# Seven products per feed-forward block: two of the weight sums made by accumulating transfers, and the products reordered

## The chip, the cores and the metric

The kernel runs on one core of a Trainium2 chip. The metric is the device time of one execution in microseconds (us), the median of three runs. Smaller is better.

## The reference

Two decoder layers (a gated linear attention and a block-sparse softmax attention) act on one sequence of 256 tokens and 1024 features in float32. Each ends in a SwiGLU feed-forward part, and that part alone is touched by the change:

```python
D_MODEL, SEQ, DEPTH = 1024, 256, 2
FFN_HIDDEN = 2816
def swiglu_ffn(x, w_gu, w_down):
    gate, up = jnp.split(x @ w_gu, 2, axis=-1)
    return (jax.nn.silu(gate) * up) @ w_down
...
x = layer_norm(DEEPNORM_ALPHA * x + swiglu_ffn(x, ffn_w_gu[i], ffn_w_down[i]), ln_g[i, 1], ln_b[i, 1])
```

## The kernel before, in words

**Products in three parts.** Every float32 operand is split into a rounded high half and the rest. ScalarE (ACT) makes the high half with a cast, VectorE (DVE) subtracts it from the raw tile to make the low half, and TensorE (PE) adds three products (high by high, low by high, high by low) into one PSUM bank. So each weight tile of 512 KB (128 partitions by 1024 numbers) costs one transfer, one cast on ACT and one subtraction on DVE before PE may use it. `split_unit` (lines 507 to 511) does this for the blocks of this case.

**Blocks of the feed-forward part.** `ffn` walks the 2816 hidden columns in blocks of the kinds "PSSSSH" (line 654): one plain block of 512 columns, four blocks of 512 columns by `seven` (lines 538 to 618), and one of 256. The four are called blocks 1 to 4 here, by the number b in the code. In each, the two halves of the tokens, the two halves of the 1024 features and the pair gate and up form a product of 2x2 matrices of blocks, and seven products take the place of eight. Each product needs one weight operand of two tiles, q = 0 and 1: the letters A to G in tile names. A is W(0,0) as loaded (the first number is the half of the features, the second 0 for gate and 1 for up), C is W(1,0) and E is W(1,1); the other four are sums. B = A + W(0,1), D = B + W(1,1) and G = D + W(1,0) are made in place in the two tiles named A. F = W(0,1) + W(1,1) is made in the two tiles loaded with W(0,1). Raw tiles other than A are all named X. The left operands are `a00`, `a01` and `a11`, which are pieces of the input, and `s1` to `s4`, which are sums of pieces. The results land in the PSUM banks pa, pc and pb, and move through `keep_` and a few element-wise steps into two tiles e (e1 and e2). PE transposes these (tile tr, lines 607 and 617), and the halves of the transposed tiles (hT) are the left operands of the down-projection (`down_now`, weights d0 to d21, banks fy) of this block, which is issued inside the next block.

**Two ways to add.** `add_to` loads the other operand as raw tiles X and adds with DVE (line 571). `add_dma` (lines 574 to 578) issues a transfer from GpSimd's queue (POOL) that adds what it reads from memory to the tile where it lands (`accum_op`), so that nothing is loaded for that sum alone. Such a transfer must wait until all that read the raw tile before are done.

**What sets the order.** Every step is recorded as an operation with an engine, an estimated duration and the buffers it touches. `Plan.emit` (lines 105 to 188) then walks a model of the five engines: of the operations that are ready it takes the one with the earliest start, then the one recorded earliest, with a small preference for those marked urgent. The result is one fixed order per engine, and each engine works through its own order without overtaking. Big tiles share 41 slots (kind "S"); a load on the SP queue waits until its slot is free. The plan's own estimates set the order alone, never a time on the chip. A load counts 512/330 us of SP's time and lands 2.3 us later (line 235). An accumulating transfer counts 1.3 us of POOL's time and lands 8.0 us later:

```python
    def dma_add(fn, reads, writes, **kw):
        return pl.op("POOL", 1.3, fn, reads, writes, extra=8.0, **kw)
```

**One block, as recorded (lines 580 to 617).** Product a00 with A; DVE adds W(0,1) into A; product s1 with B; two accumulating transfers add W(1,1) into the X tiles of W(0,1); product a01 with C; DVE adds W(1,1) into A; product s2 with D; two rows of tiles of the down-projection of the block before; product s4 with E; transpose of e1; product s3 with F; the other two rows of tiles of the down-projection; DVE adds W(1,0) into A; product a11 with G; transpose of e2. So a block holds six additions on DVE (three sums of two tiles), two accumulating transfers, eight loads of W and four of d.

Of the kernel before, what the change touches and what calls it, by code (L numbers as in the profile page):

```python
# [11 lines left out]
AF = mybir.ActivationFunctionType  # L12
ALU = mybir.AluOpType
# [178 lines left out]
def kernel(ctx, tc, x, positions, gla_w_in, gla_w_gk, gla_b_gk, gla_norm_g, gla_w_out,  # L192
                      moba_w_in, moba_w_out, ffn_w_gu, ffn_w_down, ln_g, ln_b,
                      c_f32, c_i32, out):
    nc = tc.nc
# [16 lines left out]
    pl = Plan(slots)  # L212
# [24 lines left out]
    def act(n, fn, reads, writes, **kw):  # L237
        return pl.op("ACT", 0.16 + 0.00087 * n, fn, reads, writes, **kw)

    def dve(n, fn, reads, writes, fast=False, **kw):  # L240
        return pl.op("DVE", 0.14 + (0.00052 if fast else 0.00097) * n, fn, reads, writes, **kw)
# [5 lines left out]
        return pl.op("PE", cols / 2250.0 + 0.01, fn, reads, writes, **kw)  # L247

    def dma_add(fn, reads, writes, **kw):
        return pl.op("POOL", 1.3, fn, reads, writes, extra=8.0, **kw)  # L250


# [215 lines left out]
    def ffn(i, xs, T, gb, dstT, last, x32):  # L468
# [38 lines left out]
        def split_unit(name, raw):  # L507
            hi, lo = S_(name + "h", True), S_(name + "l", True)
            act(1024, lambda: nc.scalar.copy(hi.r, raw.f), [raw], [hi])  # L509
            dve(1024, lambda: nc.vector.tensor_tensor(out=lo.r, in0=raw.f, in1=hi.f, op=ALU.subtract), [raw, hi], [lo])  # L510
            return hi, lo
# [26 lines left out]
        def seven(b, c0, pend):  # L538


            pa, pc, pb = pl.buf("ps", "pa"), pl.buf("ps", "pc"), pl.buf("ps", "pb")
            e1, e2 = S_("e1"), S_("e2")

            def product(ps, left, ws, first, last_):
                st, rd = lhs(left)
                for q, (wh, wl) in enumerate(ws):
                    def f(q=q, wh=wh, wl=wl):
                        for j in range(2):
                            sh, sl_ = st(2 * q + j)
                            cs = slice(512 * j, 512 * j + 512)  # L550
                            nc.tensor.matmul(ps.f, sh, wh.r[:, cs], start=first and q == 0 and j == 0, stop=False,  # L551
                                             skip_group_check=True)
                            nc.tensor.matmul(ps.f, sl_, wh.r[:, cs], start=False, stop=False, skip_group_check=True)  # L553
                            nc.tensor.matmul(ps.f, sh, wl.r[:, cs], start=False, stop=last_ and q == 1 and j == 1,  # L554
                                             skip_group_check=True)
                    pe(6 * 512, f, rd + [wh, wl], [ps])
# [5 lines left out]
            have = {}  # L562

            def get(kh, gu):
                if (kh, gu) not in have:
                    have[kh, gu] = [load_unit(f"X{q}", unit(kh, gu, q, c0)) for q in range(2)]
                return have[kh, gu]

            def add_to(raws, kh, gu):
                for q, other in enumerate(get(kh, gu)):  # L570
                    dve(1024, lambda q=q, other=other: nc.vector.tensor_tensor(  # L571
                        out=raws[q].f, in0=raws[q].f, in1=other.f, op=ALU.add), [raws[q], other], [raws[q]])

            def add_dma(raws, kh, gu):
                for q in range(2):
                    def f(q=q):
                        nc.gpsimd.dma_start(uv(raws[q]), unit(kh, gu, q, c0), accum_op=ALU.add)  # L577
                    dma_add(f, [raws[q]], [raws[q]])

            ch = [load_unit(f"A{q}", unit(0, 0, q, c0)) for q in range(2)]  # L580
            product(pa, "a00", [split_unit(f"A{q}", ch[q]) for q in range(2)], True, False)
            keep_(pa, e1, 0)
            add_to(ch, 0, 1)
            product(pc, "s1", [split_unit(f"B{q}", ch[q]) for q in range(2)], True, False)
            keep_(pc, e2, 0)
            add_dma(get(0, 1), 1, 1)
            r3 = get(1, 0)
            product(pb, "a01", [split_unit(f"C{q}", r3[q]) for q in range(2)], True, True)
            dve(512, lambda: nc.vector.tensor_tensor(out=e1.f[:, 0:512], in0=pb.f, in1=e1.f[:, 0:512], op=ALU.add),
                [pb, (e1, 0)], [(e1, 0)], urgent=True)  # L590
            act(512, lambda: nc.scalar.activation(e1.f[:, 0:512], e1.f[:, 0:512], AF.Silu), [(e1, 0)], [(e1, 0)],
                table="silu", urgent=True)
            add_to(ch, 1, 1)
            product(pa, "s2", [split_unit(f"D{q}", ch[q]) for q in range(2)], False, False)
            keep_(pa, e1, 1)
            r4 = get(1, 1)
            down_now(pend[:2])
            product(pc, "s4", [split_unit(f"E{q}", r4[q]) for q in range(2)], False, True)
            h, l = S_(f"hT{b}h", True), S_(f"hT{b}l", True)

            def dst(i, cs):
# [3 lines left out]
            dve(512, lambda: nc.vector.tensor_tensor(out=e1.f[:, 0:512], in0=e1.f[:, 0:512], in1=e1.f[:, 512:1024],  # L605
                                                     op=ALU.mult), [(e1, 0), (e1, 1)], [(e1, 0)], urgent=True)
            transpose_split(e1, (h, l), 0, 0, skey=0, dkey=0, dstf=lambda i: dst(i, slice(0, P)))
            product(pa, "s3", [split_unit(f"F{q}", have[0, 1][q]) for q in range(2)], False, False)
            dve(512, lambda: nc.vector.tensor_tensor(out=e2.f[:, 0:512], in0=e2.f[:, 0:512], in1=pa.f,  # L609
                                                     op=ALU.subtract), [pa, (e2, 0)], [(e2, 0)], urgent=True)  # L610
            down_now(pend[2:])
# [509 lines left out]
```

## Time and profile before

| what | value |
|---|---|
| device time, median of 3 runs | 586.07 us (585.33 to 586.32) |
| the profiled execution's own time | 585.35 us |
| its span | 583.6 us |
| PE busy | 572.5 us, 98% |
| DVE busy | 504.6 us, 86% |
| ACT busy | 345.7 us, 59% |
| POOL busy | 42.7 us, 7% |
| granted TensorE clock | 0.997 of full speed (2.4 GHz) |
| bytes moved | 118.30 MB, 203 GB/s |
| loads of X by SP / by POOL, accumulating | 48 / 16, 512 KB each |

The span is the time from the first to the last instruction of the profiled execution; 1.75 us of the execution's own time lie around it. "Busy" counts the time in which an engine had at least one instruction under way. Matmuls overlap (one of 512 columns is under way for 0.39 us, and the next starts 0.23 us later), so a lost moment on PE shows in the distance between the starts of two matmuls more surely than in the busy share. The four blocks of seven products lie at about 139 to 263 us in the first layer and at about 422 to 547 us in the second.

### The profile page before, as it was taken

Reading aid. Unit: us, or ns where it says so; the run is one execution under the profiler, and the core shown is the slowest. Engines: PE = TensorE matmul, PEld = TensorE weight load, DVE = VectorE, ACT = ScalarE, POOL = GpSimd, SP = SyncE. Lnnn points to the kernel's source line nnn. Section 1 sums busy time; section 2 is a strip of 40 time slices with the busy share of each in tenths; the row PEclk is TensorE's granted clock in tenths of the full one; section 3 lists DMA queues with packets and bytes.
Section 4 is the critical chain, followed back from the end, with each engine's and each line's share of the span. In section 5 each row is a group of like instructions: output and inputs, shape, how many; then the busy total and the mean of one; then the engine's idle time right before and its main releaser. Section 6 shows DMA issues by size and latency. Waiting matters only on the chain.

```text
span 583.6 us, 8048 instructions
## 1 busy us (share of the span) xinstructions
PE 572.5 (98%) x3004; PEld 488.4 (84%) x3004; DVE 504.6 (86%) x626; ACT 345.7 (59%) x457; POOL 42.7 (7%) x39
## 2 busy tenths in 40 slices
PE   9999999999999999999999999999999999999994
PEld 8898888888878888889889999788888788888983
DVE  5899467698999999999894789888989999999926
ACT  5886465345858586876353365634595767586410
POOL 1015000010010101000000000000101000010001
PEclk9999999999999999999999999999999999999998
DMA  9984286348797877887376545626867787978201
GB/s 291 344 301 168 74 263 242 109 126 239 247 222 219 259 240 240 219 301 249 103 245 199 153 149 166 216 73 216 212 202 223 206 285 177 316 177 291 78 0 72
DMA packets 56377, 118.30 MB, mean 203 GB/s; under 512 B 5217, under 2 KB 9729, under 8 KB 56338
## 3 DMA queue, kind: packets, MB, share of 16 engines
q1 hardware_dynamic: 51554, 108.81, 55.9%
q0 software_dynamic: 4352, 8.39, 8.8%
q10 hardware_dynamic: 432, 0.59, 0.3%
q8 instruction: 23, 0.38, 0.3%
q14 instruction: 16, 0.13, 0.1%
HBM read 116.72 MB, written 1.05 MB: 202 GB/s over the span
## 4 chain that ended last, share of the span: by engine, by line
PE 75%; DVE 12%; DMA 6%; issue 3%; ACT 2%; DVEq 0%; SPq 0%; ACTq 0%
PE fy L303 6%; PE fy L301 6%; PE fy L302 6%; PE pa L554 3%; PE pa L553 3%; PE pa L551 3%; DMA d0r<-in_ffn_w_down 2%; PE y L303 2%; PE y L301 2%; PE y L302 2%; PE tr L316 2%; DVE A L571 2%; PE pc L554 2%; PE pc L551 2%; PE pc L553 2%
## 5 line engine op out<-in xcount | busy, mean ns | idle before, releaser
L571 DVE TENSOR_TENSOR A<-A,X 128x1024 f32<-128x1024 f32 x48 | 57.2, 1219 | 0.0
L577 POOL DMA_DIRECT2D X<-in_ffn_w_gu x16 | 19.6, 1263 | 206.4 <-DVE e L609 63.7
L325 ACT CAST xT<-tr 128x512 fp32r<-128x512 f32 x16 | 9.2, 590 | 32.2 <-PE tr L316 32.1
L372 POOL TENSOR_TENSOR st<-st,mhalf 128x1 f32<-128x1 f32 x8 | 7.6, 956 | 260.3 <-DVE st L370 260.3
L509 ACT CAST B0h<-A 128x1024 fp32r<-128x1024 f32 x8 | 8.4, 1053 | 9.3 <-DVE A L571 9.2
L360 DVE SCALAR_TENSOR_TENSOR r<-xn,fy 128x512 f32<-128x512 f32 x8 | 5.5, 686 | 9.7 <-PE fy L303 9.7
L509 ACT CAST C0h<-X 128x1024 fp32r<-128x1024 f32 x8 | 8.4, 1052 | 8.8 <-DMA X<-in_ffn_w_gu 8.8
L329 DVE TENSOR_TENSOR xT<-tr,xT 128x512 fp32r<-128x512 f32 x16 | 10.8, 685 | 1.3 <-ACT xT L325 0.7
L614 ACT ACTIVATE e<-pa 128x512 f32<-128x512 f32 x8 | 4.8, 599 | 11.8 <-PE pa L554 11.7
L509 ACT CAST A0h<-A 128x1024 fp32r<-128x1024 f32 x8 | 8.4, 1051 | 5.5 <-DMA A<-in_ffn_w_gu 5.4
L364 DVE BATCH_NORM_STATS2 st<-r 128x6 f32<-128x512 f32 x16 | 11.1, 693 | 0.5
L316 PEld LDWEIGHTS tr<-ident,e 128*128 128x128 f32 x64 | 7.6, 140 | 4.7 <-DVE e L615 1.9
L316 PE MATMUL tr<-ident,e 128*128 128x128 f32 x64 | 9.8, 275 | 1.7 <-DVE e L615 1.0
L382 DVE SCALAR_TENSOR_TENSOR xn<-r,st,lnb 128x512 f32<-128x512 f32 x16 | 11.3, 746 | 0.0
L509 ACT CAST C1h<-X 128x1024 fp32r<-128x1024 f32 x8 | 8.4, 1051 | 4.8 <-DMA X<-in_ffn_w_gu 4.4
L378 DVE SCALAR_TENSOR_TENSOR r<-r,st,lng 128x512 f32<-128x512 f32 x16 | 11.2, 744 | 0.0
L509 ACT CAST G0h<-A 128x1024 fp32r<-128x1024 f32 x8 | 8.4, 1050 | 4.5 <-DVE A L571 4.5
L934 DVE SCALAR_TENSOR_TENSOR og<-o,ss,sg 128x256 f32<-128x256 f32 x8 | 3.6, 478 | 8.5 <-ACT sg L896 8.5
L509 ACT CAST D0h<-A 128x1024 fp32r<-128x1024 f32 x8 | 8.4, 1053 | 3.1 <-DVE A L571 3.1
L560 ACT COPY e<-pa 128x512 f32<-128x512 f32 x16 | 9.3, 580 | 1.0 <-PE pa L554 0.9
L510 DVE TENSOR_TENSOR G1l<-A,G1h 128x1024 fp32r<-128x1024 f32 x8 | 9.8, 1222 | 0.1
L509 ACT CAST A1h<-A 128x1024 fp32r<-128x1024 f32 x8 | 8.4, 1052 | 2.4 <-DMA A<-in_ffn_w_gu 2.4
(1050 smaller groups left out, 2283.2 us busy)
## 6 DMA issues: line engine op xcount, KB each, us to landing
X<-in_ffn_w_gu SPq DMA_DIRECT2D x48, 512.0 KB, 5.0
A<-in_ffn_w_gu SPq DMA_DIRECT2D x16, 512.0 KB, 4.4
X<-in_ffn_w_gu POOLq DMA_DIRECT2D x16, 512.0 KB, 7.5
lng<-in_ln_g SPq DMA_DIRECT2D x4, 512.0 KB, 3.8
lnb<-in_ln_b SPq DMA_DIRECT2D x4, 512.0 KB, 6.1
x<-in_x SPq DMA_DIRECT2D x4, 256.0 KB, 4.6
fg00r<-in_ffn_w_gu SPq DMA_DIRECT2D x2, 512.0 KB, 7.0
fg01r<-in_ffn_w_gu SPq DMA_DIRECT2D x2, 512.0 KB, 8.3
```

The source lines that it names most:

```text
L301: nc.tensor.matmul(ps, lh, rh, start=start, stop=False)
L302: nc.tensor.matmul(ps, ll, rh, start=False, stop=False)
L303: nc.tensor.matmul(ps, lh, rl, start=False, stop=stop)
L316: nc.tensor.transpose(ps.f[:, j * P:(j + 1) * P], src.f[:, k * P:(k + 1) * P], ident.f)
L378: nc.vector.scalar_tensor_tensor(out=r.f[:, sl], in0=r.f[:, sl], scalar=st.f[:, 12:13], in1=g.f[:, sl], op0=ALU.subtract, op1=ALU.mult)
L382: nc.vector.scalar_tensor_tensor(out=xn.f[:, sl], in0=r.f[:, sl], scalar=st.f[:, 15:16], in1=b.f[:, sl], op0=ALU.mult, op1=ALU.add)
L509: act(1024, lambda: nc.scalar.copy(hi.r, raw.f), [raw], [hi])
L551: nc.tensor.matmul(ps.f, sh, wh.r[:, cs], start=first and q == 0 and j == 0, stop=False, skip_group_check=True)
L553: nc.tensor.matmul(ps.f, sl_, wh.r[:, cs], start=False, stop=False, skip_group_check=True)
L554: nc.tensor.matmul(ps.f, sh, wl.r[:, cs], start=False, stop=last_ and q == 1 and j == 1, skip_group_check=True)
L571: dve(1024, lambda q=q, other=other: nc.vector.tensor_tensor(out=raws[q].f, in0=raws[q].f, in1=other.f, op=ALU.add), [raws[q], other], [ra ...
L577: nc.gpsimd.dma_start(uv(raws[q]), unit(kh, gu, q, c0), accum_op=ALU.add)
```

## The change

In each of the eight blocks:

- W(0,1) is no longer loaded by itself. Once A is split, two accumulating transfers add W(0,1) into the A tiles, which gives B. The two additions on DVE that did this are gone.
- F is made the other way round: W(1,1), loaded once for E and for D, is split for E first, and then two accumulating transfers add W(0,1) to it. The old two, which added W(1,1) to W(0,1), are gone. So a block has four accumulating transfers instead of two, four additions on DVE instead of six, and two loads on SP fewer. W(0,1) is still read from memory, now twice and always by an accumulating transfer; the bytes read stay the same.
- The order of recording changes: product a01 with C stands before product s1 with B, and product s4 with E before the first half of the down-projection. Two element-wise steps on e1 (the addition of pb, and Silu) lose their urgent mark.
- The plan gets, for each accumulating transfer, an operation on SP of 2.4 us that issues nothing, reads nothing and writes nothing. It moves the plan's clock of SP, and so the order; the program holds no instruction for it.

```diff
     def dma_add(fn, reads, writes, **kw):
+        pl.op("SP", 2.4, lambda: None)
         return pl.op("POOL", 1.3, fn, reads, writes, extra=8.0, **kw)
...
             keep_(pa, e1, 0)
-            add_to(ch, 0, 1)
+            add_dma(ch, 0, 1)
+            product(pb, "a01", [split_unit(f"C{q}", raw) for q, raw in enumerate(get(1, 0))], True, True)
+            dve(512, lambda: nc.vector.tensor_tensor(out=e1.f[:, 0:512], in0=pb.f, in1=e1.f[:, 0:512], op=ALU.add),
+                [pb, (e1, 0)], [(e1, 0)])
+            act(512, lambda: nc.scalar.activation(e1.f[:, 0:512], e1.f[:, 0:512], AF.Silu), [(e1, 0)], [(e1, 0)],
+                table="silu")
+            r4 = get(1, 1)
             product(pc, "s1", [split_unit(f"B{q}", ch[q]) for q in range(2)], True, False)
             keep_(pc, e2, 0)
-            add_dma(get(0, 1), 1, 1)
-            r3 = get(1, 0)
-            product(pb, "a01", [split_unit(f"C{q}", r3[q]) for q in range(2)], True, True)
...
             add_to(ch, 1, 1)
+            r4s = [split_unit(f"E{q}", r4[q]) for q in range(2)]
+            add_dma(r4, 0, 1)
             product(pa, "s2", [split_unit(f"D{q}", ch[q]) for q in range(2)], False, False)
             keep_(pa, e1, 1)
-            r4 = get(1, 1)
+            product(pc, "s4", r4s, False, True)
             down_now(pend[:2])
-            product(pc, "s4", [split_unit(f"E{q}", r4[q]) for q in range(2)], False, True)
...
-            product(pa, "s3", [split_unit(f"F{q}", have[0, 1][q]) for q in range(2)], False, False)
+            product(pa, "s3", [split_unit(f"F{q}", r4[q]) for q in range(2)], False, False)
```

Line numbers of the changed kernel are one higher than before from line 250 on, but for the steps that the change moves.

**How the order on PE moves.** PE from the end of block 1's product G to block 2's product D, first layer, before (the first matmul of each group of six; tr takes e2 of block 1):

```order
L551 MATMUL pa_1614<-A0h_1464,xT_0_1086 128x512
...
L551 MATMUL pa_1614<-A1h_1475,xT_0_1086 128x512
...
L316 MATMUL tr_1635<-ident,e_0_1409 128x128 x4
L551 MATMUL pc_1644<-B0h_1548,s1hl_1228 128x512
...
L551 MATMUL pc_1644<-B1h_1572,s1hl_1228 128x512
...
L551 MATMUL pb_1665<-C0h_1528,xT_0_1086 128x512
...
L551 MATMUL pb_1665<-C1h_1538,xT_0_1086 128x512
...
L551 MATMUL pa_1614<-D0h_1622,s2hl_1250 128x512
```

And now:

```order
L552 MATMUL pa_1598<-A0h_1490,xT_0_1089 128x512
...
L552 MATMUL pa_1598<-A1h_1502,xT_0_1089 128x512
...
L552 MATMUL pb_1623<-C0h_1521,xT_0_1089 128x512
...
L317 MATMUL tr_1633<-ident,e_0_1426 128x128 x4
L552 MATMUL pb_1623<-C1h_1536,xT_0_1089 128x512
...
L552 MATMUL pc_1651<-B0h_1596,s1hl_1228 128x512
...
L552 MATMUL pc_1651<-B1h_1610,s1hl_1228 128x512
...
L552 MATMUL pa_1598<-D0h_1647,s2hl_1252 128x512
```

C moved ahead of B, and the transpose six matmuls later, into the middle of C.

**How the order on DVE moves, at the end of block 1.** DVE up to the two steps on e1 that the transpose of e1 needs (lines 603 and 605 before, 604 and 606 now), before:

```order
L266 TENSOR_TENSOR d2l_1449<-d2r_1405,d2h_1433 128x1024
L266 TENSOR_TENSOR d3l_1462<-d3r_1421,d3h_1447 128x1024
L571 TENSOR_TENSOR A_0_1127<-A_0_1127,X_0_1260 128x1024
L571 TENSOR_TENSOR A_0_1132<-A_0_1132,X_0_1263 128x1024
L510 TENSOR_TENSOR A0l_1496<-A_0_1444,A0h_1464 128x1024
L510 TENSOR_TENSOR G0l_1506<-A_0_1127,G0h_1484 128x1024
L510 TENSOR_TENSOR G1l_1508<-A_0_1132,G1h_1498 128x1024
L510 TENSOR_TENSOR A1l_1518<-A_0_1451,A1h_1475 128x1024
L603 TENSOR_TENSOR e_0_1373<-pc_1377,e_0_1373 128x512
L605 TENSOR_TENSOR e_0_1373<-e_0_1373 128x512
```

And now:

```order
L572 TENSOR_TENSOR A_0_1141<-A_0_1141,X_0_1190 128x1024
L511 TENSOR_TENSOR G0l_1447<-A_0_1126,G0h_1430 128x1024
L511 TENSOR_TENSOR F1l_1462<-X_0_1285,F1h_1452 128x1024
L604 TENSOR_TENSOR e_0_1380<-pc_1395,e_0_1380 128x512
L606 TENSOR_TENSOR e_0_1380<-e_0_1380 128x512
L267 TENSOR_TENSOR d2l_1488<-d2r_1405,d2h_1460 128x1024
L267 TENSOR_TENSOR d3l_1498<-d3r_1424,d3h_1472 128x1024
L511 TENSOR_TENSOR G1l_1504<-A_0_1141,G1h_1476 128x1024
L511 TENSOR_TENSOR A0l_1514<-A_0_1438,A0h_1490 128x1024
L511 TENSOR_TENSOR A1l_1531<-A_0_1450,A1h_1502 128x1024
```

The two steps on e1 moved ahead of d2, d3, G1 and the splits of the next block's A.

**How the order on DVE moves, at the start of block 2.** What follows the ten rows above, now (line 616 is the step on e2 that the transpose of e2 needs; before, lines 571 to 615, the additions stood where the waiting for B stands now):

```order
L511 TENSOR_TENSOR C0l_1547<-X_0_1486,C0h_1521 128x1024
L610 TENSOR_TENSOR e_0_1426<-e_0_1426,pa_1344 128x512
L511 TENSOR_TENSOR C1l_1556<-X_0_1500,C1h_1536 128x1024
L511 TENSOR_TENSOR E0l_1566<-X_0_1512,E0h_1564 128x1024
L511 TENSOR_TENSOR E1l_1582<-X_0_1529,E1h_1580 128x1024
L511 TENSOR_TENSOR B0l_1606<-A_0_1438,B0h_1596 128x1024
L616 TENSOR_TENSOR e_0_1426<-e_0_1426 128x512
L511 TENSOR_TENSOR B1l_1621<-A_0_1450,B1h_1610 128x1024
L572 TENSOR_TENSOR A_0_1438<-A_0_1438,X_0_1512 128x1024
L572 TENSOR_TENSOR A_0_1450<-A_0_1450,X_0_1529 128x1024
```

C and E are split ahead of B; line 616 stands behind B0l, which now follows a transfer that adds.

## Rows read from the trace of the kernel before

**Rows 1.** The page, busy time of each engine

```profile
PE 572.5 (98%) x3004; PEld 488.4 (84%) x3004; DVE 504.6 (86%) x626; ACT 345.7 (59%) x457; POOL 42.7 (7%) x39
```

**Rows 2.** Windows, one per block of the first layer; columns named in its first line

```profile
core 0: us, PE busy (x) PEld busy (x) DVE busy (x) ACT busy (x) POOL busy (x), PEclk, DMA share, GB/s
139.00:170.00 31.00, 30.40 (x139) 24.92 (x138) 28.65 (x30) 21.89 (x25) 2.41 (x2) 1.00 0.73 221
...
201.50:232.40 30.90, 30.90 (x142) 25.56 (x141) 30.86 (x32) 21.30 (x25) 2.44 (x2) 1.00 0.80 236
```

**Rows 3.** Waits of PE: engine, line, releaser: total us, times, longest

```profile
PE tr L316 <- DVE e L615: 1.0, 2, 0.6
PE tr L316 <- DVE e L605: 0.6, 1, 0.6
```

**Rows 4.** Timeline of PE: start us, us under way, around the four transposes

```profile
162.27 0.39 PE L303 MATMUL fy<-d2l,hT0h 128*128 128x512 f32 x1
163.25 0.63 PE L316 MATMUL tr<-ident,e 128*128 128x128 f32 x4 [0.60 <-DVE e L605]
...
173.06 0.39 PE L554 MATMUL pa<-A1l,xT 128*128 128x512 f32 x1
174.04 0.33 PE L316 MATMUL tr<-ident,e 128*128 128x128 f32 x1 [0.60 <-DVE e L615]
...
445.77 0.39 PE L303 MATMUL fy<-d2l,hT0h 128*128 128x512 f32 x1
446.23 0.30 PE L316 MATMUL tr<-ident,e 128*128 128x128 f32 x1
...
456.21 0.39 PE L554 MATMUL pa<-A1l,xT 128*128 128x512 f32 x1
457.02 0.33 PE L316 MATMUL tr<-ident,e 128*128 128x128 f32 x1 [0.42 <-DVE e L615]
```

**Rows 5.** Timeline of PE: spacing in the stream, and a transpose that waits for nothing

```profile
150.25 0.39 PE L301 MATMUL fy<-d0h,hT0h 128*128 128x512 f32 x1
...
155.69 0.39 PE L551 MATMUL pc<-E0h,s4hl 128*128 128x512 f32 x1
...
158.41 0.39 PE L551 MATMUL pa<-F0h,s3hl 128*128 128x512 f32 x1
...
235.66 0.39 PE L554 MATMUL pa<-A1l,xT 128*128 128x512 f32 x1
235.89 0.60 PE L316 MATMUL tr<-ident,e 128*128 128x128 f32 x4
236.25 0.48 PE L551 MATMUL pc<-B0h,s1hl 128*128 128x512 f32 x1
```

**Rows 6.** Timeline of DVE ahead of the first late transpose

```profile
152.61 1.22 DVE L266 TENSOR_TENSOR d2l<-d2r,d2h 128x1024 fp32r<-128x1024 f32 x1
153.74 1.22 DVE L266 TENSOR_TENSOR d3l<-d3r,d3h 128x1024 fp32r<-128x1024 f32 x1
...
161.69 0.69 DVE L603 TENSOR_TENSOR e<-pc,e 128x512 f32<-128x512 f32 x1
162.41 0.69 DVE L605 TENSOR_TENSOR e<-e 128x512 f32<-128x512 f32 x1
```

**Rows 7.** The page, group of the additions on DVE and of the accumulating issues

```profile
L571 DVE TENSOR_TENSOR A<-A,X 128x1024 f32<-128x1024 f32 x48 | 57.2, 1219 | 0.0
L577 POOL DMA_DIRECT2D X<-in_ffn_w_gu x16 | 19.6, 1263 | 206.4 <-DVE e L609 63.7
```

**Rows 8.** The page, DMA queues: packets, MB, share of 16 engines

```profile
q1 hardware_dynamic: 51554, 108.81, 55.9%
q0 software_dynamic: 4352, 8.39, 8.8%
```

**Rows 9.** DMA issues by window, us to landing: 131 to 135, 447 to 449, 449 to 452

```profile
X<-in_ffn_w_gu POOLq DMA_DIRECT2D x1, 512.0 KB, 9.6
...
d4r<-in_ffn_w_down SPq DMA_DIRECT2D x1, 512.0 KB, 3.2
X<-in_ffn_w_gu POOLq DMA_DIRECT2D x1, 512.0 KB, 6.8
...
X<-in_ffn_w_gu POOLq DMA_DIRECT2D x2, 512.0 KB, 8.1
d5r<-in_ffn_w_down SPq DMA_DIRECT2D x1, 512.0 KB, 7.3
```

**Rows 10.** Timeline: an accumulating pair on POOL and the DVE pair it followed

```profile
227.37 2.35 DVE L571 TENSOR_TENSOR A<-A,X 128x1024 f32<-128x1024 f32 x2
...
229.23 2.44 POOL L577 DMA_DIRECT2D X<-in_ffn_w_gu  x2 [29.74 <-DVE A L571]
```

**Rows 11.** Tile B0h: the cast, duration ns min/median/max

```profile
L509 ACT CAST B0h<-A x8: 1049/1054/1055, 126.6 to 511.7; 128x1024 fp32r<-128x1024 f32 x8
```

More of the change, by code (lines that the diff above doesn't have):

```diff
@@ L582, in seven @@
             keep_(pa, e1, 0)
-            add_to(ch, 0, 1)
+            add_dma(ch, 0, 1)
[5 more added lines that the diff above has]
+            r4 = get(1, 1)
             product(pc, "s1", [split_unit(f"B{q}", ch[q]) for q in range(2)], True, False)
             keep_(pc, e2, 0)
-            add_dma(get(0, 1), 1, 1)
-            r3 = get(1, 0)
-            product(pb, "a01", [split_unit(f"C{q}", r3[q]) for q in range(2)], True, True)
[L589 to L592, printed above, removed]
             add_to(ch, 1, 1)
+            r4s = [split_unit(f"E{q}", r4[q]) for q in range(2)]
+            add_dma(r4, 0, 1)
             product(pa, "s2", [split_unit(f"D{q}", ch[q]) for q in range(2)], False, False)
             keep_(pa, e1, 1)
-            r4 = get(1, 1)
+            product(pc, "s4", r4s, False, True)
             down_now(pend[:2])
-            product(pc, "s4", [split_unit(f"E{q}", r4[q]) for q in range(2)], False, True)
             h, l = S_(f"hT{b}h", True), S_(f"hT{b}l", True)
```

## Prediction

> **What bounds the kernel now.** I read the busy times first: PE is busy for 572.5 of 583.6 us [rows 1], so the most that any edit beside PE's own work can win is what PE loses. The windows by block show who stands nearest to it: in block 3 PE is busy for all of 30.90 us and DVE for 30.86, while the DMA engines are busy for 0.80 of it, all at full clock [rows 2]. So PE sets the pace, DVE runs at the same pace without a pause, and the transfers have a fifth of their time left. The waits of PE then tell where DVE holds PE up: only at transposes of e, 1.0 and 0.6 us in all [rows 3]. The timeline gives the true size of these losses. In the stream 24 matmuls take 155.69 - 150.25 = 5.44 us, so one takes 0.227 us [rows 5], and a transpose that waits for nothing starts 0.23 us after the matmul ahead of it and lets the next one start 0.36 us later [rows 5]. The four late transposes start 0.98, 0.98, 0.46 and 0.81 us after theirs [rows 4]: 0.75 + 0.75 + 0.23 + 0.58 = 2.3 us lost. All four lie in block 1 of a layer or at its end. For the first of them DVE shows why: its instructions follow each other without a break from d2 at 152.61 to line 605 at 162.41 [rows 6], although product E, which line 603 needs, ended when F began at 158.41 [rows 5], some 3 us before line 603. So at most 2.3 us (0.4%) of this stage can be won by relief of DVE; 0.2% (1.17 us) is about what a measurement of this kernel tells from no change.
>
> **What the change takes away.** Sixteen additions on DVE, two per block. One lasts 1.22 us [rows 7] and the next starts 1.13 us after it (153.74 - 152.61, a subtraction of the same shape [rows 6]), so a block's DVE work falls by 2.3 us, from 30.9 to 28.6. None of it is on PE's path except where the four transposes wait. Sixteen loads on SP go too; SP issues the rest earlier or waits for slots as before, and I price that at nothing, since loads lead their use by several us.
>
> **What it adds: DMA time.** The queue shares price a transfer. Plain: 55.9% of 583.6 us for 108.81 MB [rows 8], which is 3.0 us per MB and 1.57 us for 512 KB. Accumulating: 8.8% for 8.39 MB [rows 8], 6.1 us per MB, 3.21 us for 512 KB. A block held 12 plain and 2 accumulating ones: 18.8 + 6.4 = 25.3 us, 0.82 of 30.9, against 0.80 read [rows 2]. It will hold 10 and 4: 15.7 + 12.8 = 28.5 us, 0.92. That is still under PE's 30.9, so by itself it costs nothing; its cover is the fifth of DMA time that was idle, and most of this cover goes. POOL issues four times 1.26 us [rows 7] in 30.9; nothing else is queued there inside the blocks, and the steps of the layer norm stand before and after them in POOL's order. The casts on ACT and the matmuls stay the same in number.
>
> **What it adds: a wait.** B now needs an accumulating transfer where it needed an addition of 1.22 us. The order says what lies in front and behind; block 2 has the least room. Let PE start its A at time 0. Between the end of block 1's E and time 0 PE has d0 and d1, a transpose, F, d2 and d3, and G: 72 matmuls and 0.36 us, 16.7 us. DVE goes through two steps on e1 (0.7 us each), d2, d3, G1 and A0 (1.13 us each) after E, 5.9 us; with 0.3 us for the hand-over, which is my choice, A0 is split at -10.5. POOL starts 0.64 us after the DVE instruction that frees the tile (229.23 less 227.37 and 1.22 [rows 10]), at -9.9. On the other side, D must be ready when PE has done A, C, a transpose and B: 36 matmuls and 0.36 us, at 8.5. From B0l on, DVE has five instructions of 1.13 us (B0l, B1l, two additions, D0l) and three short ones of 0.7 us: 7.8 us. So B0l must start by 0.7, and with the cast before it (1.05 us [rows 11]) the first transfer must have landed by -0.3: **9.6 us after its issue**. The rows have landings of 6.8 us, 8.1 as the middle of a pair, and 9.6 at the worst [rows 9]. I take 8.1, as the new transfers are pairs too. That leaves 1.5 us, and the wait costs PE nothing. The range is kept from 6.8 (2.8 us left) upward.
>
> The Trainium skill would leave more room: "DMA: Bandwidth & Descriptors", section "Anatomy of one DMA — SWDGE (gpsimd) path", fits 2.0 us plus the bytes at 436 GB/s for a transfer of GpSimd's queue, an estimate of 3.2 us for 512 KB. By that the wait would be over 6 us early and the first rival below would have no chance. The rows [rows 9] are two to three times as long, and I go by them.
>
> **The moved steps.** Between E and the transpose of e1 stood F and half of d2, 18 matmuls, 4.1 us; now it is d0 and d1, 5.4 us, and its two steps stand ahead of d2, d3, G1 and A on DVE. The transpose of e2 had A, 12 matmuls; now it has 18, 4.1 us, but line 616 stands behind B0l. E now follows B with only D between (2.7 us), and adds into the bank from which ACT must first copy B's result; that copy stands behind the cast of d4 on ACT. d4 landed 3.2 us after its issue [rows 9], and I price this at nothing. The empty operation of 2.4 us on SP issues nothing. Since it depends on nothing, the plan can place it wherever SP would wait, at the start of the program too; it may shift transposes outside the blocks. I take 0, with bounds of -0.3 and +0.8 us (the worst single late transpose [rows 4]).
>
> **The sum.** The four late transposes go: -2.3 us; I leave 0.3 of it for hand-overs, so -2.0. The profiled execution took 585.35 us and would take 583.35. The median of the runs shown, 586.07, is 0.72 above that execution, so the forecast is **584.1 us**. PE's stream cannot shrink further, so this case reaches from 583.0 to 584.9.
>
> **Rivals.** *The transfers for B land late (slower).* Place: B0l of blocks 2 and 4 in both layers; it decides from 9.6 us after issue. Block 4 has twelve instructions on DVE between A0l and B0l and is about as tight; block 3 has some 2 us more. Two accumulating transfers beside one plain load need 2 x 3.21 + 1.57 = 8.0 us of the engines, and such a trio landed at 8.1 and 7.3 us [rows 9], so they do share. Beside three plain loads it would be 2 x 3.21 + 3 x 1.57 = 11.1 us, 1.5 us too late, four times: +6.0 - 2.0 = +4.0, 590.1 us. For it: 0.92 of DMA time is close to full, and d5 took 7.3 us beside accumulating transfers where d4 took 3.2 [rows 9]. Against it: two loads per block are gone from just the stretch ahead of B. The Trainium skill speaks for it: "DMA: Bandwidth & Descriptors", section "Issuing engines are not separate DMA queues", says that transfers issued by GpSimd interleave with all others on the same 16 engines. The trace agrees in the trio just named.
>
> *Half the gain (no change).* B0l lands in time for D but holds line 616 back, so the transposes of e2 stay late (0.75 + 0.58) and only those of e1 go: -1.0, 585.1 us. For it: line 616 stands right behind B0l. Against it: it has 18 matmuls of cover where it had 12. To this case belongs that DVE's relief is eaten by idling at B0l.
>
> *The change isn't what it says.* The empty operations change the order far from the blocks. Price 0 to +0.8, inside the cases above.
>
> **How the numbers follow.** The gain of 2.0 gets 0.46, the half gain or none 0.27, the late transfers 0.27; these are also the chances of faster, same and slower by the 0.2% named above. I put the forecast highest because the chain has 1.5 us left by the rows and DVE gains 2.3 us per block, but no higher, because all that can be won is 2.3 us while each microsecond of lateness is paid four times or more. The range goes from 583.0 (all 2.3 us won, and a run 0.7 below the median, as the lowest was) to 590.1 (the late transfers at their price), which leaves out rather less than 2 in 10.
>
> **What would show it.** Right: DVE busy for about 28.6 us of a block with pauses ahead of B0l, additions 32 instead of 48, PE without waits at transposes of e, DMA share near 0.92, accumulating landings of 7 to 9 us. Wrong: PE waiting for D, B or E, or ACT waiting at B0h for a DMA while PE stands; landings of 10 us and more; or blocks of more than 31 us.

## The result, and the profile after

The changed kernel took **589.34 us** (median of eight runs, 586.79 to 592.14); the kernel before, run beside it eight times, took 585.50. The ratio is 1.0072, with a 95% interval of 1.0050 to 1.0093: slower by 3.8 us, where 584.1 was forecast. The profiled execution took 588.89 us, with a span of 587.1, 3.5 us more than before.

Four things came out as forecast: the work of DVE, the price of a transfer, the DMA share and the four transposes. The page of the changed kernel has the engines' busy times, the group of the additions, and the DMA queues (packets, MB, share of 16 engines):

```profile
PE 573.4 (98%) x3004; PEld 488.6 (83%) x3004; DVE 488.3 (83%) x610; ACT 343.1 (58%) x457; POOL 62.0 (11%) x55
...
q1 hardware_dynamic: 47202, 100.42, 50.7%
q0 software_dynamic: 8704, 16.78, 17.3%
...
L572 DVE TENSOR_TENSOR A<-A,X 128x1024 f32<-128x1024 f32 x32 | 38.5, 1220 | 0.1
```

The additions fell from 48 to 32 and DVE's busy time by 16.3 us [rows 1, 7]. An accumulating transfer takes 17.3% of 587.1 us, divided by 32, which is 3.17 us of the 16 engines; 3.21 was forecast [rows 8]. The windows from product A on, one per block of layer 1, answer to [rows 2]: DVE has 28.51 us on average where it had 30.9, the DMA share is 0.84 to 0.97, and PE loses 0.26 us in 123.6:

```profile
core 0: us, PE busy (x) PEld busy (x) DVE busy (x) ACT busy (x) POOL busy (x), PEclk, DMA share, GB/s
139.50:170.40 30.90, 30.90 (x142) 25.58 (x141) 27.77 (x28) 18.93 (x22) 3.64 (x3) 1.00 0.87 236
170.40:201.30 30.90, 30.90 (x142) 25.58 (x141) 29.66 (x29) 21.48 (x25) 4.85 (x4) 1.00 0.84 231
201.30:232.20 30.90, 30.64 (x139) 25.04 (x138) 27.89 (x29) 21.33 (x25) 4.81 (x4) 1.00 0.97 241
232.20:263.10 30.90, 30.90 (x141) 25.46 (x140) 28.71 (x30) 24.64 (x29) 2.41 (x2) 1.00 0.91 276
sum 123.60, PE 123.34 PEld 101.66 DVE 114.03 ACT 86.39 POOL 15.71; mean PE 30.83 PEld 25.41 DVE 28.51 ACT 21.60 POOL 3.93
```

The four late transposes of [rows 4] are on time. So the gain is in this execution: from the start of A in block 1 to its start in block 3, PE takes 61.78 us in layer 1 and 62.54 in layer 2, where the kernel before takes 63.38 and 63.24, which is 2.3 us less. What took it back stands, for the most part, in the first of these rows of PE's waits (engine, line, releaser: total us, times, longest); the second is two other transposes, of e2 of blocks 2 and 4 in layer 1:

```profile
PE pc L552 <- ACT e L561: 2.7, 1, 2.7
...
PE tr L317 <- DVE e L616: 0.8, 2, 0.5
```

The first row is product E of block 3 in layer 2. PE's timeline there (start us, us under way, engine, line, output and inputs; in brackets the idle time and what ended it):

```profile
497.22 0.39 PE L304 MATMUL fy<-d8l,hT2h 128*128 128x512 f32 x1
500.31 0.80 PE L552 MATMUL pc<-E0h,s4hl 128*128 128x512 f32 x1 [2.70 <-ACT e L561]
500.90 0.63 PE L554 MATMUL pc<-E0h,s4hl 128*128 128x512 f32 x1
501.33 0.63 PE L555 MATMUL pc<-E0l,s4hl 128*128 128x512 f32 x1
...
503.03 0.60 PE L552 MATMUL pc<-E1h,s4hl 128*128 128x512 f32 x1
503.46 0.41 PE L554 MATMUL pc<-E1h,s4hl 128*128 128x512 f32 x1
503.71 0.40 PE L555 MATMUL pc<-E1l,s4hl 128*128 128x512 f32 x1
```

The first matmul of E starts 3.09 us after the one ahead of it instead of 0.23. The next seven distances are 0.59 and then 0.43 us, not 0.23: 512 columns in 0.43 us is the lower of the clock's two levels, 1.2 GHz. They take 3.15 us, 1.5 more than at full speed. Then PE runs at 0.23 again. The windows say the same of the clock:

```profile
490.00:500.00 10.00, 7.61 (x34) 5.94 (x32) 8.77 (x9) 6.36 (x9) 1.20 (x1) 1.00 0.92 264
500.00:510.00 10.00, 9.69 (x36) 7.88 (x37) 8.89 (x10) 6.53 (x8) 2.44 (x2) 0.83 0.85 213
```

So one wait costs 2.9 + 1.5 = 4.4 us. The starts of product A in blocks 3 and 4 agree. They are 35.6 us apart now:

```profile
484.59 0.40 PE L552 MATMUL pa<-A0h,xT 128*128 128x512 f32 x1
...
520.19 0.40 PE L552 MATMUL pa<-A0h,xT 128*128 128x512 f32 x1
```

They were 31.15 us apart before:

```profile
485.45 0.40 PE L551 MATMUL pa<-A0h,xT 128*128 128x512 f32 x1
...
516.60 0.40 PE L551 MATMUL pa<-A0h,xT 128*128 128x512 f32 x1
```

The span is 3.5 us longer: 4.4 us here, less the 2.3 won, and 1.4 us outside the blocks named so far, 0.6 of it ahead of block 1 of layer 1 and 0.8 from block 3 of layer 1 to block 1 of layer 2.

ACT's timeline in block 3 of layer 2 shows why the copy of B's result (line 561) came so late:

```profile
493.04 0.63 ACT L588 ACTIVATE e<-e 128x512 f32<-128x512 f32 x1 [0.86 <-DVE e L586]
495.88 1.05 ACT L266 CAST d11h<-d11r 128x1024 fp32r<-128x1024 f32 x1 [2.21 <-DMA d11r<-in_ffn_w_down]
496.84 1.04 ACT L510 CAST G0h<-A 128x1024 fp32r<-128x1024 f32 x1
497.79 1.04 ACT L510 CAST F0h<-X 128x1024 fp32r<-128x1024 f32 x1
498.73 1.04 ACT L510 CAST D1h<-A 128x1024 fp32r<-128x1024 f32 x1
499.68 0.58 ACT L561 COPY e<-pc 128x512 f32<-128x512 f32 x1
```

ACT stood 2.2 us for d11, and its order has three more casts ahead of the copy. B had ended with the matmul of 495.86. The load of d11 went out at 487.82, 1.7 us behind the first accumulating transfer for F (486.15), and landed 8.0 us later; before, d11 took 3.3. In block 3 of layer 1 of the changed kernel d11 landed after 3.2 us, ACT had one cast and not three between d11's and the copy, and E, six matmuls behind B there too, did not wait. The page's list of DMA issues (KB each, median us to landing) shows the same of the weights:

```profile
X<-in_ffn_w_gu SPq DMA_DIRECT2D x32, 512.0 KB, 5.8
A<-in_ffn_w_gu SPq DMA_DIRECT2D x16, 512.0 KB, 6.4
A<-in_ffn_w_gu POOLq DMA_DIRECT2D x16, 512.0 KB, 7.3
X<-in_ffn_w_gu POOLq DMA_DIRECT2D x16, 512.0 KB, 7.8
```

Before, the two kinds of SP's loads had 5.0 and 4.4.

This is one execution. In the eight runs time and mean granted clock go together: 586.79 us at 0.996, 592.14 us at 0.988. A difference of 0.008 over 588 us is 4.7 us of work at full speed, most of the 5.35 between these two, which suggests that how often the clock falls differs from run to run. The three executions at 0.995 or more took 586.8 to 588.0, so 1.3 to 2.5 us of the loss are there without these falls.

### The profile page after: what moved, and what is told of

Read it like the earlier page. It is cut to its first block, busy times and chain, and to the rows that moved or that the text cites. A ratio compares the mean times of both kernels' runs of the same rounds, so it can differ in the third digit from the quotient of the medians.

```text
span 587.1 us, 8042 instructions
## 1 busy us (share of the span) xinstructions
PE 573.4 (98%) x3004; PEld 488.6 (83%) x3004; DVE 488.3 (83%) x610; ACT 343.1 (58%) x457; POOL 62.0 (11%) x55
## 3 DMA queue, kind: packets, MB, share of 16 engines
q0 software_dynamic: 8704, 16.78, 17.3%
## 4 chain that ended last, share of the span: by engine, by line
PE 45%; DVE 4%; DMA 3%; ACT 2%; issue 1%; DVEq 0%; ACTq 0%
PE fy L304 4%; PE fy L302 4%; PE fy L303 4%; PE pa L555 2%; PE pa L554 2%; PE pa L552 2%; DMA d11r<-in_ffn_w_down 1%; DMA A<-in_ffn_w_gu 1%; PE tr L317 1%; PE mq L302 1%; PE mk L302 1%; PE mk L303 1%; PE mq L304 1%; PE mk L304 1%; PE mq L303 1%; PE v L302 1%
## 5 line engine op out<-in xcount | busy, mean ns | idle before, releaser
L572 DVE TENSOR_TENSOR A<-A,X 128x1024 f32<-128x1024 f32 x32 | 38.5, 1220 | 0.1
L578 POOL DMA_DIRECT2D A<-in_ffn_w_gu x16 | 19.5, 1264 | 100.2 <-DVE A0l L511 67.4
L510 ACT CAST B0h<-A 128x1024 fp32r<-128x1024 f32 x8 | 8.4, 1050 | 12.8 <-DMA A<-in_ffn_w_gu 12.2
L511 DVE TENSOR_TENSOR F1l<-X,F1h 128x1024 fp32r<-128x1024 f32 x8 | 9.8, 1221 | 3.1 <-ACT F1h L510 3.1
L511 DVE TENSOR_TENSOR B0l<-A,B0h 128x1024 fp32r<-128x1024 f32 x8 | 9.8, 1223 | 1.9 <-ACT B0h L510 1.9
L510 ACT CAST D1h<-A 128x1024 fp32r<-128x1024 f32 x8 | 8.4, 1050 | 4.9 <-DVE A L572 4.7
L511 DVE TENSOR_TENSOR A0l<-A,A0h 128x1024 fp32r<-128x1024 f32 x8 | 9.8, 1221 | 1.3 <-ACT A0h L510 1.3
L511 DVE TENSOR_TENSOR F0l<-X,F0h 128x1024 fp32r<-128x1024 f32 x8 | 9.8, 1220 | 0.7 <-ACT F0h L510 0.7
```

The costliest lines, as they stand in the source:

```text
L572: dve(1024, lambda q=q, other=other: nc.vector.tensor_tensor(out=raws[q].f, in0=raws[q].f, in1=other.f, op=ALU.add), [raws[q], other], [ra ...
```

## The experiments

**The theories.** One: the time is lost where PE's E waits behind a copy on ACT, and in the clock after it. Two: the accumulating transfers take the DMA engines' time from the loads, wherever the lateness then comes out. Three: the empty operations on SP spoil the order. Each result is set against the runs of the kernel before that were made beside it (585.1 to 585.6 us).

### Moving the copy, halving the transfers, leaving out the empty operations, E late

*e1: one instruction of ACT moved; all else keeps its order.* Of the finished order, the copy of block 3 in layer 2 is taken ahead of four casts:

```diff
-        for o in order:
+        for o in hoist(self, order, (6,), 4):
             for b in o.made:
...
```

> The changed kernel with one instruction moved on one engine: in block 3 of layer 2 ACT copies B's result (line 561) ahead of the casts of d11, G0, F0 and D1 instead of behind them; every other engine keeps its order. Theory one (the time went at this place: E waits for a copy that stands behind a late load on ACT, and the clock falls after the pause): the row of PE's product E waiting for ACT line 561, 2.7 us, goes; D1 may wait in its place, at most about 1.5 us, since its cast now follows the copy; with a clock that stays full the time is 585 to 587, against 589.3 of the changed kernel. Theory two (the transfers as such cost the time, everywhere): no change, 588.5 to 590. Theory three (the empty operations and the plan's order): no change either.

Measured: 588.92 us (+3.6). The row of E is gone, and others have come (waits of PE):

```profile
PE tr L317 <- DVE e L616: 1.7, 3, 0.9
...
PE pa L555 <- DVE D1l L511: 0.7, 1, 0.7
PE tr L317 <- DVE e L606: 0.7, 1, 0.7
...
PE pa L552 <- ACT D1h L510: 0.4, 1, 0.4
```

The last three lie within 11 us of E's start: D1's cast now comes behind the copy and d11's, and the transpose of e1 is late in turn. From A to A this block still takes 34.05 us. The first row lies, but for 0.16 us, in other blocks. So the copy alone is not the cause: ACT is late as a whole, and PE waits at whichever instruction it needs next. Theory one falls in its narrow form.

*e2: each accumulating transfer moves half of its rows, in the same order.*

```diff
-                        nc.gpsimd.dma_start(uv(raws[q]), unit(kh, gu, q, c0), accum_op=ALU.add)
+                        nc.gpsimd.dma_start(uv(raws[q])[:, 0:1], unit(kh, gu, q, c0)[:, 0:1], accum_op=ALU.add)
```

> The changed kernel with the same order of instructions, but each accumulating transfer of lines 582 and 596 moves half of its rows, 256 KB instead of 512; so A and F hold only half of their second weights, and everything behind them is computed from that. Theory one (d11 lands late because it shares the DMA engines with the accumulating pair): d11 lands after 3 to 5 us instead of 8.0, ACT's wait of 2.2 us for it goes, E's wait falls from 2.7 us to 0.7 at most, and the time is 583.5 to 585. Rival (the order alone is too tight, wherever d11 lands): E still waits 2 us or more and the time stays above 588.

Measured: 583.68 us (ratio 0.9968 to 1.0003). With not one instruction moved, the changed kernel's surplus of 3.8 us is gone, and 1.6 us more. ACT's timeline at the same place:

```profile
492.17 1.03 ACT L266 CAST d11h<-d11r 128x1024 fp32r<-128x1024 f32 x1
...
495.96 0.57 ACT L561 COPY e<-pc 128x512 f32<-128x512 f32 x1
```

The same casts run without a pause, the copy is in time, and PE has no wait for E. Seen from the start of A, d11's cast is 3.0 us earlier: the load landed after 5.9 us, not 8.0 (3 to 5 were expected), and it went out 1.1 us earlier. So in this order the bytes of the transfers decide, as theory two says.

*e3: no empty operations.*

```diff
     def dma_add(fn, reads, writes, **kw):
-        pl.op("SP", 2.4, lambda: None)
```

> The changed kernel without the empty operation on SP. In its order block 3 of layer 1 gets what block 3 of layer 2 has: the casts of d11, G0, F0 and D1 ahead of the copy of B's result. Theory one: the wait and the fall of the clock, 4.4 us together in the changed kernel, come twice, or at least in both layers in part: 590 to 594. Rival (the empty operations cost time through the order they give): faster than the changed kernel, 587 or less.

Measured: 589.59 us (+4.3), near the changed kernel and just under the range of theory one. E waits in four blocks, two of each layer, without a fall of the clock (0.997 in this execution):

```profile
PE pc L551 <- ACT e L560: 3.4, 4, 1.1
```

*e4: E behind the first half of the down-projection, as before.*

```diff
-            product(pc, "s4", r4s, False, True)
             down_now(pend[:2])
+            product(pc, "s4", r4s, False, True)
```

> The changed kernel with product E recorded behind the first half of the down-projection again, as it was before; both accumulating transfers and the order C, B stay. Theory one (E too close behind B): at least 18 matmuls, 4 us, stand between B and E, no wait of E for line 561, no fall of the clock in the blocks, 583.5 to 585. Theory two (the accumulating transfers): 587 or more, with PE waiting for B, D or F behind a transfer.

Measured: 585.08 us, ratio 1.0001 (0.9983 to 1.0019): no wait for E, and the loss is gone with full transfers too. By the medians, so is the gain. The profiled execution (584.22 us, 0.9 below the median) shows the gain: from A of block 1 to A of block 4 the two layers together take 2.6 us less than before. About 1.3 us come back outside, 1.2 of them as a wait of PE for a transpose (line 616) behind block 4 of layer 1. *e8* is the same without the empty operations:

> Product E recorded late and no empty operations on SP: the order of the blocks is nearly the same in both layers. If the empty operations are worth nothing: 585.1, as with them, within 0.7. If they cost something through the order far from the blocks: 584.2 or less, which would be faster than before.

Measured: 585.10 us (0.9970 to 1.0016). The empty operations are worth nothing that can be told; theory three falls.

### E's place and the transfers, apart

*e5: the new order alone, the sums as before.*

```diff
-            add_dma(ch, 0, 1)
+            add_to(ch, 0, 1)
...
-            add_dma(r4, 0, 1)
+            add_dma(get(0, 1), 1, 1)
...
```

> Only the new order of the products: C before B, E straight behind D; the sums are made as before (W(0,1) loaded, two additions on DVE for B, one accumulating pair for F), so a block holds 12 plain and 2 accumulating transfers, 25.3 us, and 48 additions again. Theory one (E early costs only where transfers land late and hold ACT up): E waits for line 561 0.5 us in all at most, DVE is full again and some transposes of e are late, and the time is that of before within 1 us, 584.5 to 586.5. Rival (E early costs by itself): E waits for line 561 in several blocks, 2 us and more in all, and the time is 588 or more.

Measured: 588.61 us (+3.3, 1.0033 to 1.0066). The rival won: E early can cost with a DMA share of 0.79 and 0.75 (blocks of layers 1 and 2) too. But this is not the changed kernel's order: the plan put E0 straight behind B1 in four of the eight blocks, where the changed kernel has 6 to 18 matmuls between them. These are the four where PE waits, 3.1 us in all:

```profile
PE pc L552 <- ACT e L561: 3.1, 4, 1.0
```

PE's timeline at the first of them, then ACT's:

```profile
179.18 0.39 PE L555 MATMUL pc<-B1l,s1hl 128*128 128x512 f32 x1
180.33 0.50 PE L552 MATMUL pc<-E0h,s4hl 128*128 128x512 f32 x1 [0.77 <-ACT e L561]
```

```profile
179.17 0.63 ACT L588 ACTIVATE e<-e 128x512 f32<-128x512 f32 x1 [0.52 <-DVE e L586]
179.71 0.57 ACT L561 COPY e<-pc 128x512 f32<-128x512 f32 x1
```

Here the copy stands behind an activation that waits for DVE, which is full again. *e11* has the edits of e4 and e5, so E is recorded late:

> Of the whole change only C before B, with two additions on DVE and loads as before, and E recorded late: 25.3 us of transfers and 30.9 us of DVE per block. If the exchange of C and B costs and gains nothing by itself: 585.3 as before, within 0.7. If C before B is what makes DVE or ACT late: 587 or more.

Measured: 591.44 us (+5.9). Neither reading fits: the plan still put E0 straight behind B1 in the same four blocks, and E waits there for 4.9 us in all. So this pair does not say what C before B costs alone, nor what E's place costs in the changed kernel's own order. It does say that recording a step late doesn't place it late.

*e7: E late, transfers halved (the edits of e2 and e4).*

> Product E recorded late, as in the run before, and each accumulating transfer of lines 582 and 596 with half of its rows (A and F hold half of their second weights). With E late the changed kernel took 585.1, with half transfers and E early 583.7. If the full transfers still cost something with E late: 583 to 584.3, faster than before. If E's place was all: 585.1 as with full transfers, within 0.5.

Measured: 583.26 us, ratio 0.9967 (0.9945 to 0.9990), 2.0 us faster than before: the first reading, that the full transfers still cost something with E late, 1.8 us against e4. The profiled executions of e4 and e7 have spans of 582.4 and 582.3 us, so no trace shows where these 1.8 lie. That stays open.

*e6: the new pair into A alone; F as before.*

```diff
-            add_dma(r4, 0, 1)
+            add_dma(get(0, 1), 1, 1)
...
```

> The changed order with the new accumulating pair into A alone; F is made as before from a load of W(0,1) and an accumulating W(1,1). A block then holds 12 plain and 4 accumulating transfers, 12 x 1.57 + 4 x 3.21 = 31.7 us of the DMA engines beside 30.9 us of PE, and 32 additions. Theory one (the engines' time decides): the DMA share of the blocks reaches 0.97 or more, loads land late everywhere, PE waits behind casts in most blocks, and the time is 590 to 600. Rival (E's place decides and the transfers don't): as the changed kernel, 587 to 590, or less.

Measured: 595.24 us (+10.0), inside the first range. The DMA share of layer 1's blocks is 0.87 to 0.96, not the 0.97 expected. With 31.7 us of transfers for 30.9 us of PE, waits stand in B, D, E and at transposes; the longest of PE's (in the slowest of the six executions, 599.24 us):

```profile
PE tr L317 <- DVE e L616: 3.4, 2, 2.7
PE pc L552 <- ACT e L561: 3.0, 2, 1.5
PE pc L552 <- ACT B1h L510: 2.5, 1, 2.5
```

*e16, e17: the changed kernel, one pair halved.* The edit for A's pair; F's has the other tile in its place:

```diff
-                        nc.gpsimd.dma_start(uv(raws[q]), unit(kh, gu, q, c0), accum_op=ALU.add)
+                        nc.gpsimd.dma_start(uv(raws[q])[:, 0:2 - (raws is ch)], unit(kh, gu, q, c0)[:, 0:2 - (raws is ch)], accum_op=ALU.add)
```

> The changed kernel, same order, with half the rows in the accumulating pair into A alone (A holds half of its second weights behind product A). 3.2 us of the engines' time per block go, from 28.5 to 25.3. If the pair into A is what makes B's casts and those behind them late: 585 or less, and ACT's waits for a DMA at B0 nearly go. If it is the pair into F: 587.5 to 589, E's wait behind the late d11 in block 3 of layer 2 stays.

> The changed kernel, same order, with half the rows in the accumulating pair into F alone. If the pair into F delays the loads of d beside it, and with them ACT: d11 of block 3, layer 2, lands in 5 us or less, E's wait is 0.7 us at most, and the time is 585 or less. If it is the pair into A: 587.5 to 589, and ACT's waits for a DMA at B0 stay. If both are at about 586, it is the sum of bytes and not one pair.

Measured: 587.57 us with A's pair halved (+2.5), 584.69 with F's (-0.4, 0.9970 to 1.0008). By the medians F's pair is worth about 4.3 us, A's about 1.4. The pages show it in the loads beside them. With A's pair halved the loads of A on SP land as late as in the changed kernel, and X's after 5.9 us:

```profile
A<-in_ffn_w_gu SPq DMA_DIRECT2D x16, 512.0 KB, 6.3
```

With F's pair halved they land nearly as early as before the change, and X's after 5.1:

```profile
A<-in_ffn_w_gu SPq DMA_DIRECT2D x16, 512.0 KB, 4.8
```

With F's pair halved ACT still waits 13.2 us for A's transfers at B0's casts, and PE doesn't mind; inside the blocks only E (block 4 of layer 2) and a transpose (0.2 us) keep it waiting:

```profile
PE pc L552 <- ACT e L561: 0.6, 1, 0.6
```

The single load d11 does not tell the pairs apart: it landed after 5.7 us with A's pair halved and 5.9 with F's, not within the 5 expected, and E in block 3 of layer 2 waits 0.5 us or not at all. The trace with A's pair halved is of the fastest of its twelve executions (584.88 us), so it does not show where the 2.5 us lie.

### Other ways out

*e9: E in a bank of its own.*

```diff
-            product(pc, "s1", [split_unit(f"B{q}", ch[q]) for q in range(2)], True, False)
+            product(pc, "s1", [split_unit(f"B{q}", ch[q]) for q in range(2)], True, True)
...
-            product(pc, "s4", r4s, False, True)
+            pd = pl.buf("ps", "pd")
+            product(pd, "s4", r4s, True, True)
...
```

> The changed kernel with product E in a bank of its own: it no longer waits for ACT to copy B's result, and DVE adds it with one more instruction of 0.7 us per block (28.6 becomes 29.3). Theory one (what E's early place costs is its wait behind the copy): no wait of E for line 561 in any block, 584.5 to 586.5. Theory two (E early draws ACT's and DVE's other work out of step with late transfers, whichever instruction then waits, as when the copy alone was moved): PE waits for D, F or the transposes of e instead, 587 to 590.

Measured: 588.92 us (+3.3). It is theory two of that text: E no longer waits, and the waits move to F (2.0 us, and 1.1 more for F's own low half), which adds into the bank from which D's result is copied. The longest wait of PE, and ACT's timeline there, where that copy stands behind a late load:

```profile
PE pa L552 <- ACT e L561: 2.0, 1, 2.0
```

```profile
253.31 1.04 ACT L266 CAST u51h<-u51r 128x1024 fp32r<-128x1024 f32 x1 [3.91 <-DMA u51r<-in_ffn_w_gu]
254.27 0.58 ACT L561 COPY e<-pa 128x512 f32<-128x512 f32 x1
```

*e15: the plan told of later landings.*

```diff
-        return pl.op("SP", kb / 330.0, fn, reads, writes, extra=2.3, **kw)
+        return pl.op("SP", kb / 330.0, fn, reads, writes, extra=4.5, **kw)
...
-        return pl.op("POOL", 1.3, fn, reads, writes, extra=8.0, **kw)
+        return pl.op("POOL", 1.3, fn, reads, writes, extra=10.0, **kw)
```

> The changed kernel, with the plan's time from issue to landing raised by 2.2 us for loads (3.9 to 6.1 us for 512 KB) and by 2 us for accumulating transfers, near the landings that its trace shows. If the order was bad because the plan believed in earlier landings: E waits less, 585 to 587. If not, since each order leaves some instruction behind a late load: 588 or more.

Measured: 587.60 us (+2.0, between the two ranges). It is better than the changed kernel and worse than before: three waits of 0.6 to 1.5 us remain, at E, B and D.

*e13, e14: the change in block 1 only, with E late and E early.*

```diff
+            if b == 1:
...
+                add_dma(ch, 0, 1)
...
+                add_dma(r4, 0, 1)
...
+            else:
...
+                add_to(ch, 0, 1)
```

> The new way of making A and F, with C before B and E recorded late, in block 1 of each layer alone; blocks 2 to 4 as before the change. DVE is relieved where its late steps held PE up (2.3 us in the trace before), and 12 plain and 2 accumulating transfers stay in the other blocks. If the gain lies in block 1 and the loss in the transfers of blocks 2 to 4: the late transposes at the end of block 1 go, 582.8 to 584.3, faster than before. If the transfers of block 1 alone cost as much as they bring, or the lateness only moves into block 2: 585 or more.

> As e13, with E recorded early in block 1. In the profile of the changed kernel block 1 had no wait of E in either layer. If E's early place costs only where late loads hold ACT up: as e13 within 0.5 us. If it costs wherever it stands: 1 us and more above e13.

Measured: 586.90 us (ratio 1.0004 to 1.0051) and 585.28 us (0.9981 to 1.0016). Neither wins the 2 us, and E early is not worse here. In each profile one of the four transposes is still late (1.0 and 0.4 us), and e14 waits 1.3 us in the attention of layer 2, far from the change, where the kernel before waited 0.3.

*e10, e12: the two additions for B on GpSimd, recorded in the order of before and in that of e11.*

```diff
-                    dve(1024, lambda q=q, other=other: nc.vector.tensor_tensor(
+                    (gps if kh == 0 else dve)(1024, lambda q=q, other=other: (nc.gpsimd if kh == 0 else nc.vector).tensor_tensor(
```

> The kernel before with the two additions per block that make B moved from DVE to GpSimd: DVE 28.6 us per block, as after the change, and not one transfer more. If the relief of DVE is worth the 2.0 us of the prediction and GpSimd's addition hides: 582.5 to 584. If GpSimd is too slow or takes DVE's time (its longest copy in the trace before took 6.7 us for 256 columns, its shortest 0.4): PE waits for B, and the time is 586 or more.

> C before B, E late, and the two additions for B on GpSimd, with the loads of before: 28.6 us of DVE and 25.3 us of transfers per block. If GpSimd's additions hide: 582.5 to 584, and as good as or better than with B in front of C, since the additions have product C's 5.4 us more. If not: 586 or more.

Measured: 601.78 and 599.57 us (+16.2 and +14.0). (The room that e12 gives the additions is product C, twelve matmuls, 2.7 us and not the 5.4 of its text.) The page's groups of e10 (mean ns behind the busy time) show both prices: 3.4 us on GpSimd, and DVE's instructions beside it stretched from 1.2 to 2.3 us:

```profile
L571 POOL TENSOR_TENSOR A<-A,X 128x1024 f32<-128x1024 f32 x16 | 53.4, 3355 | 160.7 <-DVE A0l L510 160.7
...
L510 DVE TENSOR_TENSOR C0l<-X,C0h 128x1024 fp32r<-128x1024 f32 x8 | 18.5, 2314 | 0.0
```

The Trainium skill, "GPSIMD Engine Reference", section "Engine selection", calls an elementwise operation with two inputs about twice as slow on GpSimd; here it is 3.36 against 1.22 us, 2.8 times. Its section "Specifications" says that GpSimd shares its SBUF interfaces with VectorE, and the stretched instructions agree.

No version that computes everything beats the kernel before by more than can be told. e4, e8 and e14 are level with it.

## Why the prediction was wrong, by its steps

- **The relief of DVE (-2.0 us): right.** 48 additions became 32, DVE's work fell to 28.5 us per block, and the four late transposes went: 2.3 us in the changed kernel's own trace, 2.6 in that of e4. e7, with E late and the transfers halved, is 2.0 us faster than before by the medians; it also moves fewer bytes than the kernel before, so part of this may be due to that. No median of a kernel that computes everything shows the gain.
- **The DMA terms: right in size.** 3.17 us per transfer, shares of 0.84 to 0.97 in layer 1's blocks (0.92 forecast), median landings of 7.3 and 7.8 us where 8.1 was taken. The page of the Trainium skill that the prediction named ("DMA: Bandwidth & Descriptors", the SWDGE path) led to an estimate of 3.2 us for a landing; the measurement decides against it.
- **"That is still under PE's 30.9, so by itself it costs nothing": failed.** The sum under 30.9 says that the transfers end within the block, not when each lands. The loads beside the transfers took longer: X 5.8 us, A 6.4, d11 8.0 in the stalled block. Halving F's pair alone brings X to 5.1 and A to 4.8. The order has a part in it: X took 5.7 in e5 with the transfers of before, and 5.1 in e4 with the new ones. Halving all the transfers gives back 5.5 us with E early and 1.8 with E late.
- **"I price this at nothing" (E behind the copy of B's result): failed.** I read one block, where D's 2.7 us lay between B and E and the cast ahead of the copy had a load that landed in 3.2 us. The sum had 0 for the moved steps, +0.8 at most; this step alone cost 4.4 us in the profiled execution. The order differs from block to block: 12 matmuls between B and E in three, 18 in three, six in block 3 of either layer. In block 3 of layer 2 the six (1.4 us) met four casts ahead of the copy, the first behind a load of 8.0 us. Recording E late takes about 4 us off the changed kernel (e4).
- **The clock: missing from the sum.** A stand of 2.9 us was followed by seven slow steps, 1.5 us; the spread of the eight runs goes with the granted clock, as their ends show.
- **The rival "transfers for B land late" came near in number (590.1) by luck and was wrong in place.** ACT does wait for A's transfers at B0, 12.2 us in all, but no wait of PE in the changed kernel stands at B, and by the medians halving F's pair recovers three times what halving A's does. The price lay in the pair that I had only counted as engine time.
- **The empty operations (0): right**, by e3 and e8.

Shown: the loss needs both the full transfers, F's pair above all, and E recorded early. Take away either, and the changed kernel is level with the one before (e2, e17; e4). Removing the single wait behind the copy (e1) or the shared bank (e9) does not remove it. Not shown: that in the other executions the time goes at similar waits in other blocks; how much the changed kernel's order costs with the transfers of before, since e5 and e11 have another order; and where the 1.8 us between e4 and e7 lie.

## What to carry to other kernels

Work moved from an engine to accumulating transfers was paid twice here: in the DMA engines' time, where a transfer cost twice the plain load (3.17 against 1.57 us), and in the landing times of the loads beside it. In an order that is fixed beforehand, one late load on a shared in-order engine holds up everything behind it, the small PSUM copies included; so before moving a product up, look in every block at what stands ahead of the copy that frees its bank. And when a wait disappears but the time doesn't, halve the suspected traffic without changing the order.

## What the runs showed of the hardware that I had not expected

- An elementwise addition of 128 x 1024 float32 took GpSimd 3.36 us, and DVE's subtractions beside it 2.31 us instead of 1.22.
- After PE had stood for 2.9 us the granted clock fell to 1.2 GHz for the next seven steps, 1.5 us more for PE. In e1 it fell in the attention of layer 1, far from the change (0.91 on average from 40 to 60 us).
- A plain load of 512 KB can land after 8.0 us with two accumulating transfers per block as with four: of the tiles d0 to d15 the slowest took 8.0 us before (d1) and 8.0 in the changed kernel (d11 of layer 2), the quickest 3.1 in both.
